# A block sum of the pairwise weight products by an adding DMA, one block product moved up, and the transposes of the middle activations two steps later

## The chip, the core and the metric

The kernel runs on one core of a Trainium2 chip. The metric is the device time of one execution in microseconds (us). A profile is one execution recorded instruction by instruction; its times count from the first instruction of the program. TensorE (PE) multiplies, VectorE (DVE) and ScalarE (ACT) work elementwise, GpSimd (POOL) here mostly issues adding DMAs, SyncE (SP) issues all other DMAs.

## The reference

One decoder layer over 256 tokens of width 2048, in float32: a feed-forward part, a token mixer, a second feed-forward part of the same form. The change touches the two feed-forward parts alone.

```python
for l in range(DEPTH):                       # DEPTH = 1
    x = x + 0.5 * _swiglu(_rmsnorm(x, ffn1_norm[l]), ffn1_w_gu[l], ffn1_w_down[l])
    x = x + _token_mixing(_rmsnorm(x, mix_norm[l]), w_in[l], ...)
    x = x + 0.5 * _swiglu(_rmsnorm(x, ffn2_norm[l]), ffn2_w_gu[l], ffn2_w_down[l])

def _swiglu(h, w_gu, w_down):                # h: 256 x 2048, w_gu: 2048 x 11264, w_down: 5632 x 2048
    gate, up = jnp.split(h @ w_gu, 2, axis=-1)
    return (jax.nn.silu(gate) * up) @ w_down
```

## The kernel before

**Splitting.** Every float32 weight is split into two parts that TensorE multiplies fast: ScalarE rounds it to `hi` (line 116), VectorE computes `lo` = weight - `hi` (line 117). Each 128-row slice then takes three products: activation-high with `hi`, activation-high with `lo`, activation-low with `hi` (lines 158 to 160).

**Steps.** All work on weights stands in one list, `subs`, of steps of two 128-row slices (128x1024 numbers of weight). `stream` walks the list. Before the products of step i it emits the split of step i+3; `hi` and `lo` have four buffers each, so that split can start only when the products of step i-1 are over. A step brings `before` and `after` hooks around its products and a `post` hook right behind its split. Other work (transposes, splits of activations) runs as generators, "chains": `spawn(chain, phase, gap)` starts one `gap` steps later, "pre" and "mid" ahead of that step's products, "pe" behind them. Every engine works through its own instructions in the order in which they are emitted.

**Pairs.** Apart from the first chunk of each feed-forward part, two 512-column chunks of weights are multiplied together (`add_pair`): a 2x2 block part of the product is done in seven block products instead of eight, with block sums of weights and of activations, and the remaining rows of the chunks in the plain way. For `w_gu` (20 pairs in the program, "wide" below) a block has four slices, so that a block product takes two steps; for `w_down` (16 pairs, "narrow") it has two and takes one step. The block products are called by their code names: P1, Q5, S2 (in the list `heads`, whose Q5 is the product with X5, S2 the one with S2), then `p7`, `p3`, `p2`, `q4`, here P7, P3, P2, Q4. The plain steps of the second chunk are `g` (four in a wide pair; its last is followed by the gate's evacuation, `gate_evac`), those of the first chunk `u` (its last is followed by `up_evac`). The last three steps of a pair's `u` part are taken out of the list and put between the heads of the next pair. A wide pair thus runs in this order, with the previous pair's u steps in brackets:

P1 P1 [u] Q5 Q5 [u] S2 S2 [u] P7 P7 P3 P3 g P2 P2 g g g Q4 Q4 u

A block step has 6 matmuls (128x512), a plain step 12. The four weight blocks lie in the buffers `sb["11"]`, `["12"]`, `["21"]`, `["22"]` (1 MB each in a wide pair, 0.5 MB in a narrow one; the names in the profile are all `ffn_sb`). P1 reads block 11; the other blocks are then summed in place, each in a `post` hook: 11+12 (`t1_t3`, VectorE), 12+22 (`t1_t3`, an adding DMA that GpSimd issues, with block 22 read once more from memory, line 393), 11+22 (VectorE), and 21+11 (`t4`, VectorE, behind the split of P2). The three VectorE sums are line 350. `load_block(i + 1, ...)` fetches the next pair's blocks once a buffer's last reader is through.

**Results and banks.** `p6_after` and `p7_after` (lines 386, 389) copy a difference of partial sums into another bank. `up_evac` (line 461) multiplies gate and up into `m`, and spawns `to_mid`, which transposes `m` on TensorE (8 transposes, line 446) and splits it into `midt` (lines 204, 205); for the first chunk of a group of three it also copies it to `f` (line 452) and starts `combos_m`, the block sums of the middle activations (lines 288 to 292, 204, 205).

Of the kernel before, what the change touches and what calls it, by code (L numbers as in the profile page):

```python
# [13 lines left out]
OP = mybir.AluOpType  # L14
AX = mybir.AxisListType

T, D, FF = 256, 2048, 5632
KT = D // 128
# [7 lines left out]
NS, NSM = 4, 2  # L26
# [21 lines left out]
def hybrid_trunk_kernel(ctx, tc, x, ffn1_norm, ffn1_w_gu, ffn1_w_down, mix_norm, w_in, qk_gain, sinks, cmp_pos,  # L48
# [3 lines left out]
    PE, ACT, DVE, POOL = nc.tensor, nc.scalar, nc.vector, nc.gpsimd  # L52
# [5 lines left out]
    misc = [psum.tile([128, 512], F32, name=f"misc{i}") for i in range(4)]  # L58
    banks = Ring(misc)
    mains = Ring(main)  # L60

    x_sb = per.tile([128, 2, D], F32, name="x_sb")
    xT = per.tile([128, KT, 2, T], F32R, name="xT")
# [17 lines left out]
    def spawn(gen, phase, gap):  # L81
        chains.append([gen, phase, now[0] + gap])
# [113 lines left out]
    def part(t):  # L196
        return lambda kt, p, tb: t[:, kt, p, tb * 128:(tb + 1) * 128]
# [53 lines left out]
    def add_ffn(norm, w_gu, w_down, done):  # L251
        st = {}
# [25 lines left out]
        def block_buf(i, n):  # L278
            return st["sb"][n][:, :pairs[i][2] * 512]

        def load_block(i, *names):
            if i < len(pairs):
                for n in names:
                    nc.sync.dma_start(block_buf(i, n).rearrange("p (k c) -> p k c", c=512), block_src(i, n))
# [32 lines left out]
        def add_pair(w, r0, nkt, ns, c1, c2, lhs, sa, evac1, evac2):  # L317

            i = len(pairs)
            pairs.append((w, r0, ns, c1, c2))
            steps = [(k, min(SPLIT_KT, ns - k)) for k in range(0, ns, SPLIT_KT)]
            k = {}
            kw = dict(skip_group_check=True)

            def apart(h, tb):
                return lambda kt, p: lhs(ns * h + kt, p, tb)

            def combo(n):
                return lambda kt, p: st[sa][n][:, kt, p]

            def block(l, raw, bank, start=False, before=None, after=None, post=None):
                got = []
                for s0, n in steps:
                    def mm(hi, lo, s0=s0, n=n):  # L340
                        for s in range(n):
                            products(k[bank], lambda p: l(s0 + s, p), hi[:, s], lo[:, s], start and s0 + s == 0, False,
                                     **kw)
                    last = s0 + n == ns
                    got.append((n, 512, mm, before if s0 == 0 else None, after if last else None, None,
                                lambda s0=s0, n=n: st["sb"][raw][:, 512 * s0:512 * (s0 + n)], post if last else None))
                return got

            def add(dst, a, b):
                DVE.tensor_tensor(block_buf(i, dst), block_buf(i, a), block_buf(i, b), op=OP.add)  # L350

            def plain(names, c0, evac):
                wv = w[r0:r0 + 128 * nkt, c0:c0 + 512].rearrange("(k p) c -> p k c", p=128)

                def last():
                    bank = [k[n] for n in names]
                    evac(bank)
                    for b in bank:
                        mains.give(b)
                for q0 in range(2 * ns, nkt, SPLIT_KT):  # L360
                    end = q0 + SPLIT_KT == nkt

                    def mm(hi, lo, q0=q0, end=end):
                        ks = [(s, tb) for s in range(SPLIT_KT) for tb in range(2)]
                        if end:
                            ks.sort(key=lambda a: a[1])
                        for s, tb in ks:
                            products(k[names[tb]], lambda p: lhs(q0 + s, p, tb), hi[:, s], lo[:, s], False,
                                     q0 + s == nkt - 1, **kw)
                    yield (SPLIT_KT, 512, mm, None, last if end else None, wv[:, q0:q0 + SPLIT_KT], None, None)  # L370

            def p1_before():
                if i == 0:
                    more_banks()
                for n in ("a", "d", "b"):
                    k[n] = mains.take()

            def p1_after():
                ACT.activation(k["b"], k["a"], AF.Copy)

            def q5_after():
                ACT.activation(st["s5"], k["d"], AF.Copy)

            def p6_after():
                k["c"] = mains.take()
                DVE.tensor_tensor(k["c"], st["s5"], k["a"], op=OP.subtract)  # L386

            def p7_after():
                DVE.tensor_tensor(k["d"], st["s5"], k["a"], op=OP.subtract)  # L389

            def t1_t3():
                add("11", "11", "12")
                POOL.dma_start(block_buf(i, "12").rearrange("p (k c) -> p k c", c=512), block_src(i, "22"),
                               accum_op=OP.add)

            def t4():
                add("21", "21", "11")
                load_block(i + 1, "11")

            heads = [block(apart(0, 0), "11", "a", True, p1_before, p1_after, t1_t3),  # L400
                     block(combo("X5"), "11", "d", True, None, q5_after, lambda: add("11", "11", "22")),
                     block(combo("S2"), "11", "a", False, None, p6_after)]
            p7 = block(combo("S3"), "12", "a", after=p7_after, post=lambda: load_block(i + 1, "12"))
            p3 = block(combo("X3"), "22", "c", post=lambda: load_block(i + 1, "22"))
            p2 = block(apart(1, 0), "21", "b", post=t4)
            q4 = block(apart(1, 1), "21", "a", post=lambda: load_block(i + 1, "21"))
            tail = subs[-3:]
            del subs[-3:]
            for h, s in zip(heads, tail):
                for a in h:  # L410
                    add_sub(*a)
                subs.append(s)
            g, u = list(plain(("c", "d"), c2, evac2)), list(plain(("b", "a"), c1, evac1))
            for a in p7 + p3 + (g[:1] + p2 if len(steps) > 1 else p2 + g[:1]) + g[1:] + q4 + u:
                add_sub(*a)

        def more_banks():
            for b in misc[3:1:-1]:
                banks.free.remove(b)
                mains.free.insert(0, b)  # L420

        def fewer_banks():
            for b in misc[2:]:
# [10 lines left out]
        def to_mid(kt0):  # L434
            m = st["m"]
            got = []
            for half in range(2):
                while not banks.free:
                    yield "pe", 1
                b = banks.take()  # L440
                got.append(b)
                bv = b.rearrange("p (k t) -> p k t", k=2)
                for k in range(2):
                    for tb in range(2):
                        c0 = 128 * (2 * half + k)
                        PE.transpose(bv[:, k, tb * 128:(tb + 1) * 128], m[tb][:, c0:c0 + 128], ident)  # L446
            yield "pre", 1
            for half, b in enumerate(got):
                k0 = kt0 + 2 * half
                split_to(st["mid"][:, k0:k0 + 2, 0], st["mid"][:, k0:k0 + 2, 1], b.rearrange("p (k t) -> p k t", k=2))  # L450
                if kt0 == 0:
                    ACT.activation(st["f"][half], b, AF.Copy)
                banks.give(b)
            if kt0 == 0:
                spawn(combos_m(), "mid", 3)

        def up_evac(kt0):
            def f(bank):
                for tb in range(2):
                    m = st["m"][tb]  # L460
                    DVE.scalar_tensor_tensor(m, bank[tb], rstd[norm][:, tb:tb + 1], m, op0=OP.mult, op1=OP.mult)  # L461
                spawn(to_mid(kt0), "pe", 1)
            return f

        def down_evac(j, last):
# [10 lines left out]
        for gi, (a, b) in enumerate(groups):  # L476
            for c in range(a, b):
                kt0 = 4 * (c - a)
                if c == 0:
                    add_chunk(w_gu, 0, KT, 0, 512, part(xT), gate_evac, before=open_pools)  # L480
                    add_chunk(w_gu, 0, KT, FF, 512, part(xT), up_evac(kt0))
                else:
                    add_pair(w_gu, 0, KT, NS, FF + 512 * c, 512 * c, part(xT), "sax", up_evac(kt0), gate_evac)
            for j in (0, 2):
                add_pair(w_down, 512 * a, 4 * (b - a), NSM, 512 * (j + 1), 512 * j, part_of("mid", st), "sam",
                         down_evac(j + 1, gi == 3), down_evac(j, gi == 3))
# [767 lines left out]
    g = gens[0]  # L1254
# [46 lines left out]
```

## Time and profile before

| what | value |
|---|---|
| runs of the kernel | 2216.83 us median of 3 (2216.51 to 2217.94) |
| profiled execution | 2217.51 us |
| its span, first to last instruction | 2215.8 us |
| mean granted TensorE clock | 0.998 |
| first feed-forward part, mixer, second feed-forward part | about 0 to 760, 760 to 1430, 1430 to 2216 us |

A line of instructions gives start and duration in us, engine, line of the code, operation and operands (out<-in), and in square brackets how long the engine sat idle before it and what ended that. The rows of waits give total idle time, number of waits and the longest one. In the tables of stretches stand busy time (and instructions) of PE, PEld (TensorE's weight loads), DVE, ACT and POOL, the granted clock, the busy share of the 16 DMA engines, and GB/s.

### The profile page before, as it was taken

The page shows a single profiled execution, that of the slowest core. Times are in us where ns is not written, and L with a number is a line of the kernel's source. Part 1 is how long each engine was busy: PE and PEld are TensorE (multiplying, and loading weights), DVE is VectorE, ACT ScalarE, POOL GpSimd, SP SyncE. Part 2 cuts the span into 40 slices and gives each one's busy share as a digit, 9 for nine tenths or more (in the row PEclk, how much of TensorE's full clock was granted, in tenths as well). Part 3 has the DMA queues.
Part 4 walks back from the last instruction along what each step waited for, and adds up shares of the span by engine and source line. Part 5 has one row for each costly group of instructions (what it writes and reads, how often), then busy time and mean ns, then how long its engine had stood idle before and what let it go on. Part 6 is the DMA issues. An engine that isn't in the chain of part 4 may idle for free. (4 is left out here: it accounts for less than half of the span.)

```text
span 2215.8 us, 27393 instructions
## 1 busy us (share of the span) xinstructions
PE 2161.2 (98%) x10081; PEld 1794.7 (81%) x10081; DVE 1676.1 (76%) x2086; ACT 1240.1 (56%) x1664; POOL 112.8 (5%) x119
## 2 busy tenths in 40 slices
PE   8999999999999999999999999999999999999999
PEld 7777878877887899998888788888788777878877
DVE  7888897888788676666555554558878887897887
ACT  6554565565566665555555444445655565665564
POOL 0000000000000021000000110100000000000000
PEclk9999999999999999999999999999999999999999
DMA  8767766866775475444456666567577757766764
GB/s 291 212 186 220 222 184 211 266 202 189 243 218 178 138 230 149 118 112 138 124 152 188 182 183 196 176 192 238 184 218 252 223 170 248 211 197 217 243 195 143
DMA packets 232416, 434.30 MB, mean 196 GB/s; under 512 B 12808, under 2 KB 42072, under 8 KB 232280
## 3 DMA queue, kind: packets, MB, share of 16 engines
q1 hardware_dynamic: 217368, 403.17, 56.2%
q0 software_dynamic: 14912, 29.36, 7.5%
q8 instruction: 79, 1.29, 0.2%
q14 instruction: 57, 0.47, 0.1%
HBM read 430.39 MB, written 2.10 MB: 195 GB/s over the span
## 5 line engine op out<-in xcount | busy, mean ns | idle before, releaser
L117 DVE TENSOR_TENSOR lo<-raw,hi 128x1024 fp32r<-128x1024 f32 (+3 forms) x561 | 659.0, 1186 | 310.1 <-ACT hi L116 305.3
L116 ACT ACTIVATE hi<-raw 128x1024 fp32r<-128x1024 f32 (+3 forms) x561 | 569.7, 1020 | 346.7 <-PE main L160 267.5
L116 ACT ACTIVATE hi<-ffn_sb 128x1024 fp32r<-128x1024 f32 x392 | 406.8, 1057 | 310.0 <-DVE ffn_sb L350 119.7
L158 PE MATMUL main<-hi,xT 128*128 128x512 f32 (+2 forms) x1480 | 568.8, 384 | 5.0 <-ACT hi L116 5.0
L159 PE MATMUL main<-lo,xT 128*128 128x512 f32 (+2 forms) x1480 | 559.6, 378 | 10.7 <-DVE lo L117 10.5
L160 PE MATMUL main<-hi,xT 128*128 128x512 f32 (+2 forms) x1480 | 557.7, 377 | 0.0
L117 DVE TENSOR_TENSOR lo<-ffn_sb,hi 128x1024 fp32r<-128x1024 f32 x392 | 472.1, 1222 | 99.0 <-ACT hi L116 94.5
L158 PEld LDWEIGHTS main<-hi,xT 128*128 128x128 f32 x1480 | 279.0, 188 | 61.2 <-ACT hi L116 7.9
L159 PEld LDWEIGHTS main<-lo,xT 128*128 128x128 f32 x1480 | 278.6, 188 | 60.6 <-DVE lo L117 19.3
L160 PEld LDWEIGHTS main<-hi,xT 128*128 128x128 f32 x1480 | 278.4, 188 | 43.1
L350 DVE TENSOR_TENSOR ffn_sb<-ffn_sb,ffn_sb 128x2048 f32<-128x2048 f32 (+1 forms) x108 | 196.3, 1818 | 3.7
L158 PE MATMUL main<-hi,ffn_midt 128*128 128x512 f32 x356 | 138.7, 390 | 0.0
L160 PE MATMUL main<-hi,ffn_midt 128*128 128x512 f32 x356 | 138.5, 389 | 0.0
L159 PE MATMUL main<-lo,ffn_midt 128*128 128x512 f32 x356 | 138.5, 389 | 0.0
L159 PE MATMUL misc<-lo,xT 128*128 128x512 f32 x296 | 116.2, 392 | 4.0 <-DVE lo L117 4.0
L158 PE MATMUL misc<-hi,xT 128*128 128x512 f32 x296 | 115.7, 391 | 0.6 <-ACT hi L116 0.6
L160 PE MATMUL misc<-hi,xT 128*128 128x512 f32 x296 | 115.3, 389 | 0.0
L158 PEld LDWEIGHTS main<-hi,ffn_midt 128*128 128x128 f32 x356 | 66.8, 188 | 14.1 <-DVE main L389 0.3
L159 PEld LDWEIGHTS main<-lo,ffn_midt 128*128 128x128 f32 x356 | 66.8, 188 | 14.0 <-DVE lo L117 0.2
L160 PEld LDWEIGHTS main<-hi,ffn_midt 128*128 128x128 f32 x356 | 66.8, 188 | 13.9
L158 PE MATMUL misc<-hi,ffn_midt 128*128 128x512 f32 x188 | 73.5, 391 | 0.0
L159 PE MATMUL misc<-lo,ffn_midt 128*128 128x512 f32 x188 | 73.2, 389 | 0.0
(277 smaller groups left out, 2707.5 us busy)
## 6 DMA issues: line engine op xcount, KB each, us to landing
raw<-in_ffn_w_gu_dram SPq DMA_DIRECT2D x192, 512.0 KB, 6.0
ffn_sb<-in_ffn_w_gu_dram SPq DMA_DIRECT2D x80, 1024.0 KB, 5.2
raw<-in_ffn_w_down_dram SPq DMA_DIRECT2D x112, 512.0 KB, 5.4
raw<-in_w_in_dram SPq DMA_DIRECT2D x96, 512.0 KB, 3.6
raw<-in_w_in_dram SPq DMA_DIRECT2D x88, 384.0 KB, 3.3
ffn_sb<-in_ffn_w_down_dram SPq DMA_DIRECT2D x64, 512.0 KB, 4.4
ffn_sb<-in_ffn_w_gu_dram POOLq DMA_DIRECT2D x20, 1024.0 KB, 10.1
raw<-in_w_out_dram SPq DMA_DIRECT2D x32, 512.0 KB, 4.1
```

Source lines behind the costliest of these rows:

```text
L116: ACT.activation(hi, raw, AF.Copy)
L117: DVE.tensor_tensor(lo, raw, hi.bitcast(F32), op=OP.subtract)
L158: PE.matmul(o, lhs(0), hi, start=start, stop=False, **kw)
L159: PE.matmul(o, lhs(0), lo, start=False, stop=False, **kw)
L160: PE.matmul(o, lhs(1), hi, start=False, stop=stop, **kw)
L350: DVE.tensor_tensor(block_buf(i, dst), block_buf(i, a), block_buf(i, b), op=OP.add)
```

## The change

Three things change, in both feed-forward parts.

1. The sum 21+11 (`t4`) is no longer a VectorE instruction but a DMA that GpSimd issues, from one buffer to the other, with addition. The sum 12+22 was an adding DMA before, so two of the four block sums now are.
2. P2 follows S2 directly: P1 P1 [u] Q5 Q5 [u] S2 S2 P2 P2 [u] P7 P7 P3 P3 g g Q4 g Q4 g u in a wide pair. The next pair's block 11 is loaded behind the split of Q4's first step (`post0`) rather than inside `t4`, and the banks `d` and `b` are taken later.
3. `to_mid` starts 3 steps behind `up_evac` rather than 1, but for chunk 10 (the last of each feed-forward part).

```diff
             def p1_before():
                 if i == 0:
                     more_banks()
-                for n in ("a", "d", "b"):
-                    k[n] = mains.take()
+                k["a"] = mains.take()
 
             def p1_after():
+                k["b"] = mains.take()
                 ACT.activation(k["b"], k["a"], AF.Copy)
+
+            def q5_before():
+                k["d"] = mains.take()
...
             def t4():
-                add("21", "21", "11")
-                load_block(i + 1, "11")
+                POOL.dma_start(block_buf(i, "21").rearrange("p (k c) -> p k c", c=512),
+                               block_buf(i, "11").rearrange("p (k c) -> p k c", c=512), accum_op=OP.add)
 
             heads = [block(apart(0, 0), "11", "a", True, p1_before, p1_after, t1_t3),
-                     block(combo("X5"), "11", "d", True, None, q5_after, lambda: add("11", "11", "22")),
-                     block(combo("S2"), "11", "a", False, None, p6_after)]
+                     block(combo("X5"), "11", "d", True, q5_before, q5_after, lambda: add("11", "11", "22")),
+                     block(combo("S2"), "11", "a", False, None, p6_after) + block(apart(1, 0), "21", "b", post=t4)]
             p7 = block(combo("S3"), "12", "a", after=p7_after, post=lambda: load_block(i + 1, "12"))
             p3 = block(combo("X3"), "22", "c", post=lambda: load_block(i + 1, "22"))
-            p2 = block(apart(1, 0), "21", "b", post=t4)
-            q4 = block(apart(1, 1), "21", "a", post=lambda: load_block(i + 1, "21"))
+            q4 = block(apart(1, 1), "21", "a", post=lambda: load_block(i + 1, "21"),
+                       post0=lambda: load_block(i + 1, "11"))
...
-            for a in p7 + p3 + (g[:1] + p2 if len(steps) > 1 else p2 + g[:1]) + g[1:] + q4 + u:
+            m = min(2, len(g) - 1)
+            for a in p7 + p3 + g[:m] + q4[:1] + g[m:m + 1] + q4[1:] + g[m + 1:] + u:
                 add_sub(*a)
...
-        def up_evac(kt0):
+        def up_evac(kt0, gap):
...
-                spawn(to_mid(kt0), "pe", 1)
+                spawn(to_mid(kt0), "pe", gap)
...
+                up = up_evac(kt0, 1 if c == 10 else 3)
```

Line numbers behind the change are shifted: the VectorE sums are line 356, the adding DMAs lines 402 (12+22) and 406 (21+11), `p6_after` 395, `p7_after` 398, `gate_evac` 442, the transposes 456, `up_evac` 471.

On VectorE, a wide pair of the second feed-forward part from the subtraction of `p6_after` to the third plain step's split; `ffn_sb_10015`, `_10016`, `_10017` are the blocks 12, 22 and 21, `_10014` is block 11. Before:

```order
L386 TENSOR_TENSOR main_65<-ffn_s_10022,misc_70 128x512
L117 TENSOR_TENSOR lo_83<-ffn_sb_10016,hi_79 128x1024
L461 SCALAR_TENSOR_TENSOR ffn_m_10018<-main_66,rstd_ffn_95,ffn_m_10018 128x512
L461 SCALAR_TENSOR_TENSOR ffn_m_10019<-main_64,rstd_ffn_95,ffn_m_10019 128x512
L117 TENSOR_TENSOR lo_84<-ffn_sb_10016,hi_80 128x1024
L205 TENSOR_TENSOR ffn_midt<-misc_67,ffn_midt 128x2x256
L205 TENSOR_TENSOR ffn_midt<-misc_68,ffn_midt 128x2x256
L117 TENSOR_TENSOR lo_85<-raw_73,hi_81 128x1024
L389 TENSOR_TENSOR main_63<-ffn_s_10022,misc_70 128x512
L117 TENSOR_TENSOR lo_86<-ffn_sb_10017,hi_82 128x1024
L117 TENSOR_TENSOR lo_83<-ffn_sb_10017,hi_79 128x1024
L350 TENSOR_TENSOR ffn_sb_10017<-ffn_sb_10017,ffn_sb_10014 128x2048
```

The same place in the changed kernel:

```order
L117 TENSOR_TENSOR lo_83<-ffn_sb_10015,hi_79 128x1024
L117 TENSOR_TENSOR lo_84<-ffn_sb_10015,hi_80 128x1024
L117 TENSOR_TENSOR lo_85<-ffn_sb_10016,hi_81 128x1024
L471 SCALAR_TENSOR_TENSOR ffn_m_10018<-main_65,rstd_ffn_95,ffn_m_10018 128x512
L471 SCALAR_TENSOR_TENSOR ffn_m_10019<-main_66,rstd_ffn_95,ffn_m_10019 128x512
L117 TENSOR_TENSOR lo_86<-ffn_sb_10016,hi_82 128x1024
L117 TENSOR_TENSOR lo_83<-raw_73,hi_79 128x1024
L398 TENSOR_TENSOR misc_70<-ffn_s_10022,main_63 128x512
L117 TENSOR_TENSOR lo_84<-raw_74,hi_80 128x1024
L205 TENSOR_TENSOR ffn_midt<-misc_67,ffn_midt 128x2x256
L205 TENSOR_TENSOR ffn_midt<-misc_68,ffn_midt 128x2x256
L117 TENSOR_TENSOR lo_85<-ffn_sb_10017,hi_81 128x1024
```

The split of `midt` moved from ahead of the first plain step (`raw_73`) to behind the second one (`raw_74`), and the sum 21+11 is gone from this engine, as are P2's two splits from this place.

On TensorE, around the 8 transposes in such a pair (each of the four rows stands there twice in alternation with its neighbour). Before, where `ffn_saxS_10009` marks P7:

```order
L160 MATMUL misc_70<-hi_81,ffn_saxS_10009 128x512
L446 MATMUL misc_67<-ident,ffn_m_10018 128x128
L446 MATMUL misc_67<-ident,ffn_m_10019 128x128
L446 MATMUL misc_68<-ident,ffn_m_10018 128x128
L446 MATMUL misc_68<-ident,ffn_m_10019 128x128
L158 MATMUL misc_70<-hi_82,ffn_saxS_10009 128x512
```

After, where `ffn_saxX_10008` marks P3:

```order
L160 MATMUL main_64<-hi_81,ffn_saxX_10008 128x512
L456 MATMUL misc_67<-ident,ffn_m_10018 128x128
L456 MATMUL misc_67<-ident,ffn_m_10019 128x128
L456 MATMUL misc_68<-ident,ffn_m_10018 128x128
L456 MATMUL misc_68<-ident,ffn_m_10019 128x128
L158 MATMUL main_64<-hi_82,ffn_saxX_10008 128x512
```

The transposes moved from between the two steps of P7 to between the two steps of P3.

On GpSimd, the adding DMAs of one wide and the two narrow pairs behind it, in the changed kernel (before, only the rows with `in_ffn` stood there, one behind the other):

```order
L402 DMA ffn_sb_10015<-in_ffn_w_gu_dram 128x4x512
L406 DMA ffn_sb_10017<-ffn_sb_10014 128x2048
L402 DMA ffn_sb_10015<-in_ffn_w_down_dram 128x2x512
L406 DMA ffn_sb_10017<-ffn_sb_10014 128x1024
L402 DMA ffn_sb_10015<-in_ffn_w_down_dram 128x2x512
L406 DMA ffn_sb_10017<-ffn_sb_10014 128x1024
```

Each sum 12+22 is now followed by the sum 21+11 of the same pair.

More of the change, by code (lines that the diff above doesn't have):

```diff
@@ L335, in combo, with block @@
                 return lambda kt, p: st[sa][n][:, kt, p]
-            def block(l, raw, bank, start=False, before=None, after=None, post=None):
+            def block(l, raw, bank, start=False, before=None, after=None, post=None, post0=None):
                 got = []
@@ L344, in block, with posts @@
                     last = s0 + n == ns
+                    def posts(first=s0 == 0, last=last):
+                        if first and post0:
+                            post0()
+                        if last and post:
+                            post()
                     got.append((n, 512, mm, before if s0 == 0 else None, after if last else None, None,
-                                lambda s0=s0, n=n: st["sb"][raw][:, 512 * s0:512 * (s0 + n)], post if last else None))
+                                lambda s0=s0, n=n: st["sb"][raw][:, 512 * s0:512 * (s0 + n)], posts))
                 return got
@@ L413, in add_pair @@
             g, u = list(plain(("c", "d"), c2, evac2)), list(plain(("b", "a"), c1, evac1))
-            for a in p7 + p3 + (g[:1] + p2 if len(steps) > 1 else p2 + g[:1]) + g[1:] + q4 + u:
+            m = min(2, len(g) - 1)
+            for a in p7 + p3 + g[:m] + q4[:1] + g[m:m + 1] + q4[1:] + g[m + 1:] + u:
                 add_sub(*a)
         def more_banks():
-            for b in misc[3:1:-1]:
+            for b, at in ((misc[2], 0), (misc[3], 2)):
                 banks.free.remove(b)
-                mains.free.insert(0, b)
+                mains.free.insert(at, b)
         def fewer_banks():
@@ L478, in add_ffn @@
                 kt0 = 4 * (c - a)
+                up = up_evac(kt0, 1 if c == 10 else 3)
                 if c == 0:
                     add_chunk(w_gu, 0, KT, 0, 512, part(xT), gate_evac, before=open_pools)
-                    add_chunk(w_gu, 0, KT, FF, 512, part(xT), up_evac(kt0))
+                    add_chunk(w_gu, 0, KT, FF, 512, part(xT), up)
                 else:
-                    add_pair(w_gu, 0, KT, NS, FF + 512 * c, 512 * c, part(xT), "sax", up_evac(kt0), gate_evac)
+                    add_pair(w_gu, 0, KT, NS, FF + 512 * c, 512 * c, part(xT), "sax", up, gate_evac)
             for j in (0, 2):
```

## The prediction

> **What bounds the kernel now.** I read the busy times of the page first, then TensorE's waits over the whole program, then the timelines of TensorE and VectorE in one wide pair of the second feed-forward part, then the DMA tables.
>
> ```profile
> PE 2161.2 (98%) x10081; PEld 1794.7 (81%) x10081; DVE 1676.1 (76%) x2086; ACT 1240.1 (56%) x1664; POOL 112.8 (5%) x119
> 1900.00:2100.00 200.00, 196.19 (x869) 160.10 (x868) 172.09 (x161) 117.41 (x128) 6.23 (x5) 1.00 0.70 218
> ```
>
> TensorE bounds the program. The change leaves its matmuls as they are, so only its idle time, 2215.8 - 2161.2 = 54.6 us, can be won. In a stretch of 200 us of the second feed-forward part VectorE is busy for 172.09 us, with the TensorE clock at 1.00: a second engine close behind the first, so that a burst of VectorE work makes TensorE wait although VectorE is not full on average. TensorE's waits, with total us, number and longest:
>
> ```profile
> PE misc L446 <- DVE ffn_m L461: 13.0, 25, 1.4
> PE main L159 <- DVE lo L117: 10.5, 16, 0.8
> PE main L158 <- ACT hi L116: 5.0, 7, 2.9
> PE misc L159 <- DVE lo L117: 4.0, 6, 0.8
> PE misc L234 <- DVE x_sb L469: 3.5, 6, 1.3
> PE main L158 <- DVE misc L386: 2.5, 2, 1.9
> PE misc L158 <- DVE main L386: 1.4, 1, 1.4
> PE main L158 <- DVE main L386: 1.3, 2, 0.8
> ```
>
> Nearly all are waits for VectorE, inside pairs. The reader should see three families: transposes that wait for `up_evac` (L461), `lo` splits that come late (L117), and products that wait for a bank's subtraction (L386). Where they fall:
>
> ```profile
> 1944.53 0.39 PE L160 MATMUL main<-hi,ffn_saxX 128*128 128x512 f32 x1
> 1945.21 0.51 PE L158 MATMUL main<-hi,xT 128*128 128x512 f32 x1 [0.29 <-ACT hi L116]
> 1946.47 0.51 PE L159 MATMUL main<-lo,xT 128*128 128x512 f32 x1 [0.76 <-DVE lo L117]
> ...
> 1951.97 0.39 PE L158 MATMUL main<-hi,xT 128*128 128x512 f32 x1
> 1952.80 0.50 PE L159 MATMUL main<-lo,xT 128*128 128x512 f32 x1 [0.44 <-DVE lo L117]
> ...
> 1974.44 0.39 PE L160 MATMUL main<-hi,ffn_saxX 128*128 128x512 f32 x1
> 1974.67 0.39 PE L158 MATMUL misc<-hi,xT 128*128 128x512 f32 x1
> 1975.85 0.50 PE L159 MATMUL misc<-lo,xT 128*128 128x512 f32 x1 [0.79 <-DVE lo L117]
> ...
> 2022.81 0.39 PE L160 MATMUL misc<-hi,ffn_samS 128*128 128x512 f32 x1
> 2024.08 0.33 PE L446 MATMUL misc<-ident,ffn_m 128*128 128x128 f32 x1 [0.88 <-DVE ffn_m L461]
> 2024.74 0.98 PE L446 MATMUL misc<-ident,ffn_m 128*128 128x128 f32 x7 [0.33 <-DVE ffn_m L461]
> ...
> 2174.53 0.33 PE L446 MATMUL misc<-ident,ffn_m 128*128 128x128 f32 x1 [0.62 <-DVE ffn_m L461]
> 2175.19 0.99 PE L446 MATMUL misc<-ident,ffn_m 128*128 128x128 f32 x7 [0.33 <-DVE ffn_m L461]
> ```
>
> Unhindered, matmuls start 0.23 us apart (1974.44 to 1974.67), so a block step takes 6 x 0.227 = 1.36 us and a plain step 2.72 us. A wait costs more than its idle time, since the first matmul behind it restarts slowly: from 1945.21 to 1946.47 is 1.26 us, 1.03 more than 0.23, for 0.76 idle; from 2024.08 to 2024.74 about 0.55 more than a transpose's step of 0.11 (0.98 us for seven), for 0.33 idle. I count about 0.2 us on top of each wait, and about 0.27 for the `lo` waits.
>
> What VectorE does meanwhile:
>
> ```profile
> 1942.89 0.69 DVE L205 TENSOR_TENSOR ffn_midt<-misc,ffn_midt 128x512 fp32r<-128x512 f32 x1 [1.15 <-ACT ffn_midt L204]
> 1945.19 1.23 DVE L117 TENSOR_TENSOR lo<-raw,hi 128x1024 fp32r<-128x1024 f32 x1 [1.61 <-ACT hi L116]
> ...
> 1949.32 2.29 DVE L350 TENSOR_TENSOR ffn_sb<-ffn_sb,ffn_sb 128x2048 f32<-128x2048 f32 x1
> 1951.53 1.22 DVE L117 TENSOR_TENSOR lo<-raw,hi 128x1024 fp32r<-128x1024 f32 x1
> ...
> 1961.79 0.75 DVE L432 SCALAR_TENSOR_TENSOR ffn_m<-main,rstd_ffn,ffn_m 128x512 f32<-128x512 f32 x1 [0.46 <-ACT ffn_m L431]
> ...
> 1970.44 0.42 DVE L205 TENSOR_TENSOR ffn_samX<-ffn_f,ffn_samX 128x256 fp32r<-128x256 f32 x1
> ...
> 1972.37 2.29 DVE L350 TENSOR_TENSOR ffn_sb<-ffn_sb,ffn_sb 128x2048 f32<-128x2048 f32 x1
> ...
> 2022.14 1.23 DVE L350 TENSOR_TENSOR ffn_sb<-ffn_sb,ffn_sb 128x1024 f32<-128x1024 f32 x1
> 2023.28 1.40 DVE L461 SCALAR_TENSOR_TENSOR ffn_m<-main,rstd_ffn,ffn_m 128x512 f32<-128x512 f32 x2
> ```
>
> The split of the first g step (1945.19) stands behind the split of `midt`, which waits for the transposes. The second g step's split (1951.53) stands behind the sum 21+11 (1949.32). In narrow pairs that sum (2022.14) stands right ahead of `up_evac` (2023.28).
>
> **The change part by part.** The sum is made against the profiled 2217.51 us, 0.68 above the median.
>
> *Transposes.* 13.0 us idle in 25 waits, with 25 x 0.19 on top: 17.8 us. Moved two steps on, `up_evac` (1.40 us) has P7 and half of P3 as cover, 4.1 us in a wide pair; in the narrow one P7, P3 and a g step, 5.4 us. So these waits go, except behind chunk 10, where the distance stays one step: its two waits (2174.53, 2175.19) lose 0.62 + 0.33 + 2 x 0.2, 1.35 us per feed-forward part. There the sum that stood ahead of `up_evac` is gone, so I keep 0.55 of each. Gain 17.8 - 1.1 = 16.7 us.
>
> *First g step.* 0.45 (1944.53 to 1945.21, less 0.23) and 1.03 us, in the 8 pairs behind a first chunk of a group, where `midt` is also copied: 11.8 us. The `midt` split now comes after the splits of both first g steps, and next in line is Q4's; TensorE has P3, g, g = 1.36 + 5.44 = 6.8 us of split work, against 4.7 us from the wait within the `midt` split to the end of the late split in the rows above (1942.89 - 1.15 = 1941.7 to 1946.4). Gain 11.8.
>
> *Second g step.* 1951.97 to 1952.80 less 0.23 is 0.60 us, in 8 pairs: 4.8 us. The 2.29 us sum ahead of it is gone. Gain 4.8.
>
> *Products behind L386.* 2.5 + 1.4 + 1.3 us in 5 waits, with 0.19 each 6.1 us: P7 goes on in the bank that `p6_after` reads, or waits for block 12. P2, in another bank, now stands between: 1.36 or 2.72 us more. Gain 6.1.
>
> *x transposes at the end of the first part.* The `x_sb` waits, 3.5 us in 6, with 0.19 each 4.6 us; the narrow sum (1.23) stood ahead of those too. It can take away up to three times 0.9; I take 2.0.
>
> *u step behind Q5.* 1974.67 to 1975.85 less 0.23 is 0.95 us, in 6 pairs. Here VectorE comes from `gate_evac`, two block sums and the `combos_m` work, which the change shifts by four steps into this place. Counting from P1's first matmul as 0: `gate_evac` ends at 1.55 with two more `combos_m` sums (0.84) and the sum 11+12 ahead of it; then three splits at 1.25 to 5.2, the sum 11+22 to 7.5, two `combos_m` splits to 8.35, the u split to 9.6, needed at 8.39. The wait becomes 1.2: a loss of 6 x 0.25 = 1.5 us. Without `combos_m` work the same chain ends at 7.9, 0.5 us before it is needed.
>
> *The adding DMA.* It takes 20 x 2.29 + 16 x 1.23 = 65.5 us off VectorE, of which only the waits above were on the path, and adds 36 issues on GpSimd:
>
> ```profile
> ffn_sb<-in_ffn_w_gu_dram SPq DMA_DIRECT2D x80, 1024.0 KB, 5.2
> ffn_sb<-in_ffn_w_gu_dram POOLq DMA_DIRECT2D x20, 1024.0 KB, 10.1
> ffn_sb<-in_ffn_w_down_dram POOLq DMA_DIRECT2D x16, 512.0 KB, 7.2
> q1 hardware_dynamic: 8799, 17.10, 52.2%
> q0 software_dynamic: 1056, 2.10, 11.8%
> 1923.07 1.28 POOL L393 DMA_DIRECT2D ffn_sb<-in_ffn_w_gu_dram  x1 [39.87 <-DVE ffn_sb L350]
> ```
>
> An adding DMA between two on-chip buffers is not in the trace. The nearest row is the adding load of the same size, 10.1 us; a plain load of 1 MB takes 5.2. Its place: P2's splits are done about when S2's products end. From there TensorE has P2, u, P7, P3, the transposes (about 1.0), g, g: 2.72 x 6 + 1.0 = 17.3 us to Q4. Less 1.06 + 1.23 + 0.2 for Q4's split and 0.5 for the issue, the DMA may take 14.3 us before TensorE waits. Block 11 of the next pair is loaded behind Q4's split: 5.2 us, with g, Q4, g, u (9.5 us) until P1. In a narrow pair the same count allows about 12 us, against 7.2. I take 10.1 and a cost of 0. Bounds: at 5.2 still 0; at twice 10.1, 20.2 us, (20.2 - 14.3) x 20 wide pairs = +118 us. GpSimd's queue holds nothing else there, since it sat idle for 39.87 us before an issue, and the next pair's sum 12+22 comes some 30 us later. SyncE's load of block 11 waits where Q4's split waited already; P2's block 21 is loaded a step earlier than before and read six steps earlier, some 10 us before it is needed.
>
> A rule weighed: the Trainium skill, DMA: Bandwidth & Descriptors, Rules for kernel authors, says that spreading DMAs over issuing engines gives no bandwidth, because all run on the same 16 DMA engines and interleave. By that rule the new DMAs take their time from the weight loads. That hangs on the first rival below.
>
> In this kernel's numbers (the two queue rows are of the window from 1914 to 2012 us): two adding DMAs took 11.8% of 98 us, 5.8 us of all engines each, and plain loads 52.2% of 98 us for 17.10 MB, 3.0 us per MB. The 10.1 us were reached beside raw loads; the new DMA meets one block load of 1 MB more, so I expect up to 10.1 + 3.0 = 13.1 us, 1.2 us short of the edge of 14.3.
>
> *Banks.* They are taken later from a ring of six with four free at P1; a and b were freed ten steps earlier, c and d one pair part earlier, behind `gate_evac`: no cost.
>
> Sum: 16.7 + 11.8 + 4.8 + 6.1 + 2.0 - 1.5 = 39.9 us gained; 2217.5 - 39.9 = 2177.6, with the median 0.7 lower 2177. I add 3 us, 0.15 us in each of 20 wide pairs, for the stretch from P1 to u, where VectorE has only 0.5 us in hand: **2180 us**.
>
> **The rivals.**
>
> *Half the gain.* The DMA engines, already 0.70 busy, stretch the new sum to about 15.3 us, and TensorE waits 1 us in each wide pair: 20 us back, 2200 us. For it: the 13.1 us above, not far from the edge. Against it: the 20 adding loads have a median of 10.1 in the company that they have.
>
> *Slower.* One mechanism: the on-chip adding DMA takes longer than 14.3 + 39.9 / 20 = 16.3 us in wide pairs, beyond which each us costs 20. At 20.2 us it is -39.9 + 118 = +78, about 2295 us. For it: an addition already doubles a load's landing (10.1 against 5.2). Against it: here no source is read from main memory.
>
> *No change.* The waits only move, since VectorE is the real bound: 2217 us. For it, 172 of 200 us busy; against it, that leaves 28 us per 200, and 65.5 us of work goes.
>
> **How the numbers follow.** The forecast gets 0.70, with 2169 (2177 less the rest of the x waits, 2.6, and the u-step waits, 5.7) to 2192; half the gain 0.17 (2192 to 2208, 0.8 to 1.4 us per wide pair); slower 0.09; no change 0.04. The range 2170 to 2204 holds most of the first two, about 0.8. A measurement can tell about 0.2%, 4.4 us, from no change. Faster: 0.70 + 0.17 + 0.01 of the slower case = 0.88; same 0.04; slower 0.08.
>
> **What would show it.** In the profile after: L446's waits (now line 456) down from 25 to about 4; the `lo` waits from 22 to about 6, all at the u step behind Q5; no wait for the subtraction (line 395); VectorE about 65 us less busy; the new DMA landing within 14 us. The prediction is wrong if ScalarE's `hi` waits for a DMA at Q4 and TensorE behind it, or if the raw loads come late.

## The result, and the profile after

The changed kernel took 2181.59 us, median of 4 runs (2180.89 to 2184.26), against 2216.67 us for the kernel before: a ratio of 0.9843 (95% interval 0.9826 to 0.986). Timed once more beside two other versions it came to 2181.7 us, ratio 0.9839 (0.9825 to 0.9852). The profiled execution took 2181.03 us, 36.5 us less than the one before; its span is 2179.3 us.

The busy times of the page, then the second feed-forward part with the columns of the stretches:

```profile
PE 2144.9 (98%) x10081; PEld 1796.9 (82%) x10081; DVE 1615.8 (74%) x2050; ACT 1247.9 (57%) x1664; POOL 145.5 (7%) x155
1370.00:2180.00 810.00, 797.41 (x3570) 658.31 (x3568) 639.27 (x630) 466.84 (x524) 46.49 (x41) 1.00 0.77 229
```

VectorE is 60.3 us less busy, GpSimd 32.7 us more. TensorE's idle time fell from 54.6 to 34.4 us. Its busy time fell too, by 16.3 us with the same 10081 instructions. The slow restart behind each wait counts as busy, and the waits fell from 74 to 32; that the restarts make up the 16.3 us is inferred from this, not measured one by one. Some 2 us of it, by an estimate from these stretches, are the clock: behind some longer waits TensorE ran at half speed for 3.4 us twice before (from 158.0 and 192.2 us on) and once after (from 695.6 us on). TensorE's waits after, in the same view as before, without those of the mixer and of the program's start:

```profile
PE main L159 <- DVE lo L117: 6.2, 10, 0.8
PE main L158 <- DVE x_sb L479: 5.7, 2, 2.9
PE main L158 <- ACT hi L116: 3.1, 2, 2.9
PE main L158 <- DVE main L398: 1.4, 1, 1.4
PE misc L159 <- DVE lo L117: 1.1, 2, 0.6
PE misc L160 <- DVE ffn_samX L205: 1.1, 2, 0.6
PE misc L158 <- DVE misc L398: 1.1, 1, 1.1
PE misc L456 <- DVE ffn_m L471: 0.7, 2, 0.3
PE main L158 <- DVE misc L395: 0.6, 1, 0.6
PE misc L234 <- DVE x_sb L479: 0.5, 2, 0.3
```

The transposes wait twice rather than 25 times, `lo` is late 12 times rather than 22. New are products (L158) that wait for the addition to x (L479) or for `p7_after` (L398), and the row with `ffn_samX`. The DMA table:

```profile
ffn_sb<-in_ffn_w_gu_dram SPq DMA_DIRECT2D x80, 1024.0 KB, 6.9
ffn_sb<-in_ffn_w_down_dram SPq DMA_DIRECT2D x64, 512.0 KB, 6.4
ffn_sb<-in_ffn_w_gu_dram POOLq DMA_DIRECT2D x20, 1024.0 KB, 9.8
ffn_sb<-ffn_sb POOLq DMA_DIRECT2D x20, 1024.0 KB, 8.1
ffn_sb<-ffn_sb POOLq DMA_DIRECT2D x16, 512.0 KB, 4.7
q0 software_dynamic: 20096, 58.72, 15.4%
```

The new sum lands in 8.1 us (wide) and 4.7 us (narrow). The loads of blocks take longer than before, 6.9 us rather than 5.2 (wide) and 6.4 rather than 4.4 (narrow), without TensorE waiting for them in wide pairs. The experiments below part the causes: the wide loads take 6.5 us with the new order alone and 5.1 with the DMA alone, so their rise comes mostly with the order; the narrow ones take 4.9 and 4.3, 4.5 with order and delay, and reach 6.4 only when the DMA is added to these.

The longest new waits stand at the end of each feed-forward part, between its two last narrow pairs. (The two for L398 stand in narrow pairs at 154 and 189 us, and two short ones for `lo` at 53.5 and 59.4 us, all in the first part.) TensorE at the end of the second part:

```profile
2142.60 0.50 PE L159 MATMUL main<-lo,ffn_midt 128*128 128x512 f32 x1 [0.67 <-DVE lo L117]
2145.00 0.50 PE L159 MATMUL main<-lo,ffn_midt 128*128 128x512 f32 x1 [0.74 <-DVE lo L117]
2150.65 0.47 PE L158 MATMUL main<-hi,ffn_samX 128*128 128x512 f32 x1 [2.86 <-DVE x_sb L479]
```

ScalarE, and the loads on SyncE, at the same place:

```profile
2140.23 1.06 ACT L116 ACTIVATE hi<-ffn_sb 128x1024 fp32r<-128x1024 f32 x1 [3.34 <-DMA ffn_sb<-in_ffn_w_down_dram]
```

```profile
2133.71 2.98 SPq L284 DMA_DIRECT2D ffn_sb<-in_ffn_w_down_dram  x2
```

Block 11 of the last pair is loaded from 2133.71 us on, and ScalarE waits 3.34 us for it before it can split P1's weights. Everything behind that is late, up to the addition to x (L479) that has to read the bank in which Q5 is to start: 2.86 us idle. These pairs have only two g steps. Since the last three steps of a pair stand between the heads of the next, the second g step comes behind the next P1 here, so that P1 follows Q4 directly, with no step between in which block 11 could land; and the banks of that g step are still unread when Q5 takes one.

### The profile page after: what moved, and what is told of

It reads as the page before. It is cut to its first block, busy times and chain, and to the rows that moved or that the text cites. A ratio compares the mean times of both kernels' runs of the same rounds, so it can differ in the third digit from the quotient of the medians.

```text
span 2179.3 us, 27509 instructions
## 1 busy us (share of the span) xinstructions
PE 2144.9 (98%) x10081; PEld 1796.9 (82%) x10081; DVE 1615.8 (74%) x2050; ACT 1247.9 (57%) x1664; POOL 145.5 (7%) x155
## 3 DMA queue, kind: packets, MB, share of 16 engines
q0 software_dynamic: 20096, 58.72, 15.4%
## 5 line engine op out<-in xcount | busy, mean ns | idle before, releaser
L116 ACT ACTIVATE hi<-ffn_sb 128x1024 fp32r<-128x1024 f32 x392 | 412.5, 1059 | 294.5 <-PE main L160 122.6
L158 PE MATMUL main<-hi,xT 128*128 128x512 f32 (+2 forms) x1480 | 567.7, 384 | 2.9 <-ACT hi L116 2.9
L158 PEld LDWEIGHTS main<-hi,xT 128*128 128x128 f32 x1480 | 279.1, 189 | 55.0 <-issue 6.6
L158 PE MATMUL main<-hi,ffn_midt 128*128 128x512 f32 x348 | 136.3, 392 | 1.6 <-DVE main L398 1.4
L160 PE MATMUL main<-hi,ffn_midt 128*128 128x512 f32 x348 | 135.6, 390 | 0.0
L356 DVE TENSOR_TENSOR ffn_sb<-ffn_sb,ffn_sb 128x2048 f32<-128x2048 f32 (+1 forms) x72 | 130.9, 1818 | 2.5
L158 PE MATMUL misc<-hi,xT 128*128 128x512 f32 x296 | 115.3, 389 | 0.0
L159 PEld LDWEIGHTS main<-lo,ffn_midt 128*128 128x128 f32 x348 | 65.4, 188 | 17.7 <-DVE lo L117 4.5
L158 PEld LDWEIGHTS main<-hi,ffn_midt 128*128 128x128 f32 x348 | 65.4, 188 | 15.8 <-DVE main L398 1.8
L158 PE MATMUL misc<-hi,ffn_midt 128*128 128x512 f32 x196 | 76.7, 391 | 1.1 <-DVE misc L398 1.1
```

The source lines that it names most:

```text
L116: ACT.activation(hi, raw, AF.Copy)
L158: PE.matmul(o, lhs(0), hi, start=start, stop=False, **kw)
L159: PE.matmul(o, lhs(0), lo, start=False, stop=False, **kw)
L160: PE.matmul(o, lhs(1), hi, start=False, stop=stop, **kw)
```

## Experiments

**One part alone.** Three kernels hold one part of the change each.

```diff
 e1_gap: before +                    e2_order: after -                       e3_dma: before +
+ up_evac(kt0, 1 if c == 10 else 3)  + add("21", "21", "11") in t4           + t4 as POOL.dma_start(..., accum_op=OP.add)
                                     + load_block(i + 1, "11") in t4         + q4: post0=lambda: load_block(i + 1, "11")
                                     + up_evac(kt0, 1)
```

The delay of the transposes alone:

> The kernel before with one part of the change: the transposes two steps later (chunk 10 excepted). Theory (each part removes its own waits and hands the VectorE work on to the next tight place): the transposes' waits go (-15 us), the wait at the first g step goes (-12 us), but the split of midt now stands ahead of P2's second split and of the VectorE sum 21+11, so that the second g step is late by about 2 us more in 8 pairs (+16 us). Net -11 us, about 2205 us. Rival (the delay does nearly all of the gain by itself): -27 us, about 2190 us.

Measured: 2201.46 us, ratio 0.993 (0.9915 to 0.9945), 16 us less than before. TensorE's waits in it:

```profile
PE main L159 <- DVE lo L117: 14.7, 17, 1.8
PE misc L159 <- DVE lo L117: 4.8, 6, 1.8
PE misc L446 <- DVE ffn_m L461: 2.9, 4, 1.3
```

The transposes' waits fell from 25 to 4, and the waits for `lo` rose from 14.5 to 19.5 us, the longest from 0.8 to 1.8: what the `midt` split no longer delays at the first g step it delays, together with the sum 21+11, at the second (1.8 us there in all 8 pairs). The theory's mechanism holds; the gain was 16 us where it counted 11.

The new order alone:

> The kernel before with one part of the change: P2 right behind S2 and Q4 between the g steps; the sum 21+11 stays on VectorE, the transposes stay one step behind. Theory: the sum (2.29 us) now stands in the tightest stretch, ahead of up_evac, and the transposes wait about 2 us in each of 20 wide pairs (+30 us against the waits they have now), against -11 us for the second g step and the products behind the subtraction. Net slower or equal: 2216 to 2240 us. Rival (the new order is what helps): below 2200 us.

Measured: 2206.81 us, ratio 0.9954 (0.9939 to 0.9969). It was faster by 10 us where the theory had it equal or slower. Waits:

```profile
PE misc L455 <- DVE ffn_m L470: 12.1, 29, 0.5
PE main L159 <- DVE lo L117: 6.7, 22, 0.8
PE misc L159 <- DVE lo L117: 3.9, 8, 0.8
```

The waits of the transposes are there in all 14 wide pairs that hold transposes (the theory counted 20), at 0.52 and 0.33 us each, not 2: the sum on VectorE takes 2.29 us, and I counted nearly all of it as delay. Where the rest of it was taken up was not traced. The long waits of the transposes in narrow pairs and the late splits at the second g step went, and the waits for the subtraction fell from 5.2 us in 5 to 2.8 us in 2; the waits at the first g step stayed in all 8 pairs.

The adding DMA alone. Where Q4 ends a short pair in this order it stands behind the next P1, so there the load that follows Q4's split comes behind the split that needs it, and the last pair of each part multiplies the old block; the instructions are the same.

> The kernel before with one part of the change: the sum 21+11 as an adding DMA, P2 and Q4 where they were, block 11 of the next pair loaded behind Q4's first split. Theory: from P2's splits to Q4 there are only about 8 us for a DMA that lands in 8.1, and from Q4's first split to P1 only 5.4 us of products (Q4, u) for a load that lands in 6.9 us and a split; TensorE waits about 4 us in 20 wide and 2 to 3 us in 16 narrow pairs: +80 to +130 us, 2295 to 2345 us. Rival (the relief of VectorE by 65 us is what helps, wherever P2 stands): below 2205 us.

Measured: 2276.2 us, ratio 1.027 (1.0253 to 1.0287), slower by 59 us, less than expected but on that side. VectorE is busy for 1607.7 us, 68 us less than before, and TensorE waits for `lo` 62 times rather than 22:

```profile
PE main L159 <- DVE lo L117: 30.0, 38, 1.8
PE misc L159 <- DVE lo L117: 18.2, 24, 1.8
```

The new ones stand at Q4, behind the sum, and above all at the u step behind P1 (17 waits of 0.8 to 1.8 us), behind the load of block 11. Between the profiled executions (56 us) 36 are idle time and 21 longer busy time of the same instructions; the granted clock was 0.994, against 0.998 before. Less work on VectorE is worth nothing if the blocks for Q4 and for the next P1 come later than VectorE would have let them.

**One part undone.** The sum back on VectorE in the changed kernel:

> The changed kernel with one part undone: the sum 21+11 back on VectorE behind P2's split, with the load of block 11 behind it. Theory: VectorE falls behind by 2.29 us in the stretch S2 P2 u; that costs 0.2 us in most wide pairs and about 1.1 us in 6 of them (+11 us), 1 us at each of the x transposes and behind chunk 10 (+4 us), but block 11 comes early again, so the 9 us lost between the two last narrow pairs of each part come back (-9 us): about 2187 us, 2180 to 2195. Rival (the DMA is the main part of the gain): over 2200 us.

Measured: 2185.75 us, ratio 0.9859 (0.9844 to 0.9874), as the theory had it, and under the rival's 2200; the interval overlaps with that of the changed kernel. In all 20 wide pairs the u step behind P2 now waits some 0.2 us, and the late splits between the last narrow pairs are gone. The delay undone:

> The changed kernel with one part undone: the transposes one step behind up_evac again. Theory: up_evac ends 0.2 us or more after P7's first step, so the transposes wait again about 0.6 us in each of the 22 chunks (+14 us), and the split of midt stands ahead of the first g step's again (1.5 us in 8 pairs, +12 us): +20 to +28 us on the changed kernel, 2202 to 2210 us. Rival (with the sum gone from VectorE, the transposes no longer need the delay): within 5 us of the changed kernel, below 2187 us.

Measured: 2187.12 us, ratio 0.9867 (0.9854 to 0.9881). The theory was out and the rival nearly right: 5.5 us over the changed kernel, where it said at most 5, and not 20 to 28; the two intervals overlap a little, so that 5 us is not clear of noise. No wait of a transpose for `up_evac` is left in this kernel either. VectorE and TensorE at such a place in it:

```profile
1530.83 1.41 DVE L471 SCALAR_TENSOR_TENSOR ffn_m<-main,rstd_ffn,ffn_m 128x512 f32<-128x512 f32 x2
```

```profile
1532.47 1.03 PE L456 MATMUL misc<-ident,ffn_m 128*128 128x128 f32 x8
```

`up_evac` starts 0.28 us before P7's first product (1531.11) and ends at 1532.24, just before the transposes would start. Where the sum was still on VectorE (the order alone), the same instruction started at 1543.54, 1.24 us behind P7's first product (1542.30), and the first transpose waited 0.52 us. So in the new order the delay and the DMA each remove these waits without the other; in the old order the DMA alone left 15 of them, 4.8 us. What the delay adds in the changed kernel is the first g step (0.31 and 0.77 us idle in this kernel, in 8 pairs), less the u-step waits behind Q5, which this kernel does not have.

**The new waits removed.** In pairs with two g steps, the sum on VectorE and block 11 loaded at once:

```diff
+            short = nkt - 2 * ns < 8
             def t4():
+                if short:
+                    add("21", "21", "11")
+                    load_block(i + 1, "11")
+                    return
...
-                       post0=lambda: load_block(i + 1, "11"))
+                       post0=lambda: short or load_block(i + 1, "11"))
```

> The changed kernel, but in the 4 pairs with only two g steps (the two last narrow pairs of each feed-forward part) the sum 21+11 is on VectorE again, with the load of block 11 right behind it. Theory: in the changed kernel block 11 of the last pair is loaded too late there, since only Q4, g and u stand between Q4 and the next P1; the two late splits (0.84 and 0.91 us) go, and the wait of 3.0 us for the bank that the x addition reads shrinks to the 1.7 us seen where the sum was on VectorE throughout: -3 us per part, about 2176 us. Rival (the 3.0 us are due to the bank alone, and block 11 costs nothing): within 2 us of the changed kernel.

Measured: 2172.33 us, ratio 0.98 (0.9787 to 0.9814), 9 us less than the changed kernel where 6 were expected. The wait for x shrank as expected, and the late splits went with it:

```profile
PE main L158 <- DVE x_sb L485: 3.2, 2, 1.6
PE main L159 <- DVE lo L117: 2.9, 5, 0.6
```

Then `combos_m` earlier in the changed kernel, with `spawn(combos_m(), "mid", 1)` for 3 and gaps of 2 for 3:

> The changed kernel, with combos_m (the block sums of the middle activations) started one step behind the split of midt rather than three, and with gaps of two steps rather than three, so that all of it falls into the plain steps ahead of the next P1. Theory: the 0.73 us waits, at the u step behind Q5 in 6 pairs and at Q5 in 2, come from this work standing in the stretch where VectorE has no time over: 8 x 0.73 = -5.8 us, about 2176 us. Rival (the waits only move to P1): no change against the changed kernel.

Measured: 2178.23 us, ratio 0.9825 (0.9812 to 0.9839): 3 us, which the interval does not tell from the changed kernel. The trace tells where the theory was off: the waits at Q5 of the narrow pairs are gone, those at the u step shrank from 0.57 to 0.22 us idle, but did not go.

Both together, with Q4 behind both g steps in the short pairs:

> Both edits together, and in the 4 pairs with two g steps Q4 stands behind both g steps, as in the kernel before, so that the banks of g are read out one step earlier. Theory: -3 us per part for block 11, -1.7 us per part for the bank, -5.8 us for combos_m: -15 us on the changed kernel, about 2167 us. Rival (Q4's split now comes late for block 21 of the next pair, whose load follows it): the bank's gain is lost, 2172 us or more.

Measured: 2166.49 us, ratio 0.9773 (0.976 to 0.9786), 15 us less than the changed kernel, and the fastest version. TensorE's products no longer wait for a bank of x behind a narrow pair, though the x transposes wait 2.7 us again (0.5 in the changed kernel); the `lo` waits are down to 2.3 us:

```profile
PE main L159 <- DVE lo L117: 1.9, 6, 0.8
PE misc L159 <- DVE lo L117: 0.4, 2, 0.2
```

**What the DMA is worth without its side effect.** The same version with the sum on VectorE in all pairs:

> The version with Q4 behind both g steps in the short pairs and combos_m early, but with the sum 21+11 on VectorE in all pairs and the load of block 11 behind it. Theory (the adding DMA is worth what VectorE's 2.29 us cost ahead of the u step behind P2, 0.37 us in each of 20 wide pairs): +7 us on that version, about 2174 us. Rival (with the other waits gone VectorE has enough time over and the DMA is worth nothing): 2165 to 2169 us.

Measured: 2182.91 us, ratio 0.984 (0.9827 to 0.9854): 16 us more, not 7. The `lo` waits are back:

```profile
PE main L159 <- DVE lo L117: 6.8, 22, 0.8
PE misc L159 <- DVE lo L117: 2.1, 6, 0.7
```

So the DMA in itself is worth 13 to 16 us: 16 between these two, and 13 between the changed kernel with the sum on VectorE in all pairs (2185.75 us) and in the short pairs alone (2172.33). The 4 us that the undoing showed are this gain less what late block 11 costs in the short pairs. The place that the theory named was right: the u step behind P2 waits about 0.2 us in all 20 wide pairs. But those behind Q5 grew too (0.22 to 0.65 us in 6 pairs), and two waits behind a subtraction by 0.7 us each. With 0.2 us on top of each new wait these come to about 12 us; the rest was not found. The changed kernel timed beside it:

> The changed kernel unaltered, timed beside the version before it in this call so that the two can be compared on one chip: 2181 to 2183 us on either theory.

Measured: 2181.7 us, as above.

**How much slack the DMA has.** The sum of each wide pair issued in pieces, so that it lands later:

```diff
+                parts = 16 if len(steps) > 1 else 1          # 32 in the other kernel
+                wid = 512 * ns // parts
+                for q in range(parts):
+                    POOL.dma_start(block_buf(i, "21")[:, q * wid:(q + 1) * wid],
+                                   block_buf(i, "11")[:, q * wid:(q + 1) * wid], accum_op=OP.add)
```

> The changed kernel, with the sum 21+11 of each wide pair issued as 16 adding DMAs of 128 columns instead of one, which makes it land later without adding bytes. An issue took 0.89 us in the changed kernel, so the last one starts after 14 us and lands at about 17.7 us, the first half of the block at about 10.6. Theory (slack of 14.3 us to Q4's first step, 4.1 us more to its second, and a block load of 6.9 us behind it): the first half is in time, the second just in time, the load of block 11 up to 1 us late: 2181 to 2205 us. Rival (the slack is smaller than counted, and the single DMA of 8.1 us was near its edge): over 2230 us.

Measured: 2232.64 us, ratio 1.0069 (1.0046 to 1.0092), 51 us more than the changed kernel, 2.5 per wide pair; it went past the rival's 2230. The landing was the main thing that the theory had wrong. In one pair the first piece was issued at 1940.59 us and the last landed at 1961.03, 20.4 us later where 17.7 were expected. ScalarE then waits for the sum, and again for the block behind it:

```profile
1961.17 1.06 ACT L116 ACTIVATE hi<-ffn_sb 128x1024 fp32r<-128x1024 f32 x1 [2.96 <-DMA ffn_sb<-ffn_sb]
1966.24 2.01 ACT L116 ACTIVATE hi<-ffn_sb 128x1024 fp32r<-128x1024 f32 x2 [2.10 <-DMA ffn_sb<-in_ffn_w_gu_dram]
```

In this pair the second wait, for block 11, is the one that reaches TensorE, at the u step behind P1 (1.96 us idle); 10 wide pairs wait there, for 17 us in all. In 15 of the 20 TensorE also waits at Q4's second step, 15 us in all. By the theory's own count both allow a landing of about 18 us (18.4 for Q4's second step), so that both should be late at 20.4, as they are. That 20.4 passes 18 by 2.4 us and each pair lost 2.5 is in part chance: of the 53 us between the profiled executions, 33 are idle time and 20 longer busy time, with a granted clock of 0.995 against 0.999.

> The same with 32 adding DMAs of 64 columns in each wide pair: the first half lands at about 17.7 us, the second at about 32 us. Theory: Q4's first step waits 3.4 us, its second 10 us more, 13.6 us in each of 20 wide pairs, +270 us, about 2450 us (2380 to 2500). Rival (the sum is hidden far longer than 14.3 us): below 2250 us.

Measured: 2420.4 us, ratio 1.0922 (1.089 to 1.0953): +239 us, 12 per wide pair against 13.6 expected. TensorE now waits at Q4 itself, and goes on slowly behind the long waits:

```profile
PE main L158 <- ACT hi L116: 104.1, 25, 8.4
PE misc L158 <- ACT hi L116: 23.9, 8, 4.1
1952.50 0.80 PE L158 MATMUL main<-hi,xT 128*128 128x512 f32 x1 [7.74 <-ACT hi L116]
1954.78 0.63 PE L158 MATMUL main<-hi,xT 128*128 128x512 f32 x1
1955.20 0.63 PE L159 MATMUL main<-lo,xT 128*128 128x512 f32 x1
1952.50:1959.50 7.00, 6.54 (x15) 4.78 (x16) 6.97 (x6) 4.49 (x5) 0.57 (x1) 0.50 0.43 141
```

In the 7 us behind that wait the granted clock is 0.50, and matmuls start 0.42 us apart (1954.78 to 1955.20) rather than 0.23; over the whole program it is 0.960, against 0.999 in the changed kernel. So of the 241 us between the profiled executions only 151 are idle time, 7.6 us per wide pair, and 90 are longer busy time. The forecast of 13.6 us counted waits alone; that the sum came near it is partly luck.

## Why the prediction was right, and where its steps were off

The time was 2181.59 us against 2180, in the range, and its main reason holds: TensorE's matmuls are unchanged, and the gain is the waits for VectorE inside the pairs. Step by step:

- *Transposes, 16.7 us.* Right in the trace: two waits of 0.33 us are left, both behind chunk 10, as forecast. But the step gave them to the delay alone; the delay undone costs some 5 us, hardly clear of noise, since in the new order the DMA removes the same waits. The terms are not worth their numbers one by one: the delay alone gave 16 us, the order alone 10, the two together 31, and all three 35.
- *First and second g step, 11.8 and 4.8 us.* Right: those waits are gone in the wide pairs. The short pairs at the end show `lo` waits at P1 and a g step instead.
- *Products behind the subtraction, 6.1 us.* Partly wrong. P7 waits once, 0.6 us. But in narrow pairs P2 stood between P3 and the first g step; without it that g step waits for `p7_after` (L398, 1.4 and 1.1 us) in two of the 16 narrow pairs. The step looked at what P2 now separates and not at what it no longer does.
- *x transposes, 2.0 us.* Somewhat more: 3.5 us idle became 0.5.
- *u step behind Q5, -1.5 us.* The place was right, in the same 6 pairs; the wait was shorter, 0.57 us idle with 0.16 of restart, 0.73 us against 0.95 before and 1.2 forecast, so that it shrank where the step had it grow. In the pair at 1939 us the u split ended 9.06 us behind P1's first product where the step counted 9.6. Not forecast: `combos_m` also reaches into Q5 of the narrow pair (1.1 us in 2 waits).
- *The adding DMA, 0.* Right in wide pairs: 8.1 us, under the 10.1 taken. The pieces bear out the order of the count: at 20.4 us block 11 and Q4's second step are late, at 30 us Q4's first. The price per us also holds longer busy time, which the count did not have. In a narrow pair "the same count" gives by its own terms 10.3 us with four g steps and 7.5 with two, not 12; the sum landed in 4.7 us, so nothing came of it. The step failed in the short pairs: the 9.5 us between Q4 and P1 were counted for four g steps only. With two g steps nothing stands between, and the load was late; the version without it was 9 us faster.
- *Banks, no cost.* Wrong in the same place: there the ring gives Q5 a bank that the second g step has just filled, 5.7 us idle in 2 waits. (The change also alters where `more_banks` puts two banks into the ring; whether that matters here was not tried.)
- *The allowance of 3 us* for the stretch from P1 to the u step was not needed there. It stood in for part of the 9 us above, and larger gains elsewhere made up the rest. "Only its idle time, 54.6 us, can be won" was too strict as well: 16.3 us of the gain is busy time. That the sum came out within 2 us is partly luck.

Of the rivals, half the gain did not come: no DMA at Q4 was late. The rule cited with it, from the Trainium skill, DMA: Bandwidth & Descriptors, Rules for kernel authors, that DMAs of all issuing engines share the same 16 DMA engines and interleave, is borne out in part: with the DMA added to order and delay the 0.5 MB block loads went from 4.5 to 6.4 us, the 1 MB ones only from 6.4 to 6.9, and neither reached TensorE in wide pairs. The slower rival's mechanism is real, as the pieces show, but the single DMA landed in half the time that it needed.

## What to carry to other kernels

When a helper engine is nearly as busy as the bound engine, list the bound engine's waits by place and ask for each which instruction stands ahead of the late one; parts of a change that clear the same stretch are not worth the sum of their single gains. Here two of them gave more together (31 us against 16 and 10), and the delay, once the DMA was there, gave less (some 5 us against 16). Moving a sum to a DMA frees the engine but can delay the loads that reuse its buffers, so count the steps to the next reader in the shortest variant of the loop, not only in the usual one. The same holds for a ring of banks: check its order at the shortest body.

## What was not expected of the hardware

- In the changed kernel an adding DMA from one on-chip buffer to another lands sooner than an adding load of the same size: 8.1 against 9.8 us for 1 MB, 4.7 against 7.9 for 0.5 MB. It is not so in every order: in the old one (the DMA alone) the 0.5 MB sum took 8.6 us, and the adding load of that size 7.1. The 36 new DMAs took 5184 packets for 29.36 MB (20096 less 14912), 5.7 KB each, where the adding loads had 2 KB each; whether the packet size or the source makes the difference was not tried apart. Their issue took 0.89 us on GpSimd against 1.32.
- TensorE's busy time is not fixed by its instructions: 16.3 us of "busy" disappeared together with 20.2 us of idle time, and with 32 pieces some 90 us were added, with the same 10081 instructions.
- Behind some long waits TensorE ran at half speed for a while. Behind the 2.84 us wait at 695.29 us in the changed kernel matmuls started 0.43 us apart rather than 0.23 until about 699 us, with a granted clock of 0.50; behind the 2.86 us wait of the second part there was no such stretch, so the length of the wait alone does not decide it.
- Sixteen pieces of the same sum land in 20.4 to 23.4 us rather than in 8.1, 32 in about 30: small adding DMAs cost time by their number.
